# A hybrid decoder block: FOX heads 0 to 3 as a second Strassen stream, and the column steps of the inversions on GpSimd

## The chip, the cores and the metric

The kernel runs on one core of one Trainium2 chip. The metric is the device time of one execution in microseconds (us). Before the change the median of three runs is 983.41 us (983.08 to 984.17).

## What is computed

One decoder block over 512 tokens of width 1024. Two branches read the same normalised input; each has 8 heads of width 128.

```python
u = rmsnorm(x)
gq, gk, gv, gz, ga, gb, fq, fk, fv, ff, gate_a, gate_b = split(u @ w_in)
o_a = gated_delta_rule_chunked(l2norm(silu(conv(gq))), l2norm(silu(conv(gk))), silu(conv(gv)), g, beta)
y_a = (rmsnorm(o_a) * silu(gz)) @ w_proj_gdn            # GDN branch, a triangular solve in each chunk
y_b = forgetting_attention(rmsnorm(fq), rmsnorm(fk), fv, log_f) @ w_proj_fox      # FOX branch
h   = x + (sigmoid(gate_a) * y_a + sigmoid(gate_b) * y_b) @ w_out
out = h + relu(rmsnorm(h) @ w_up)**2 @ w_down
```

## The kernel before

All products are done in pairs of reduced-precision parts: an operand is split into `hi` (a cast, on ScalarE) and `lo` (the rest, a subtraction on VectorE), and three products hi*hi, lo*hi, hi*lo are summed in PSUM. `unit` (line 260) hands out the weight tiles of 128 x 1024 in the order of the list `seq`; it loads them three units ahead and splits them two units ahead (`LA_RAW`, `LA_SPLIT`). The pool `whl` holds four `hi` and four `lo` tiles, so the split of a unit waits until an earlier unit's products are over.

The program is written as a main sequence on TensorE and a set of generators (`tasks`); `tick` advances each of them by one step. A scheduler then fixes one order for each engine, and on the chip each engine works through its own list in that order.

Main sequence around the change, before: 5 `z` units, the 12 units of GDN heads 0 to 3 (`gdn_group(0)`), then `fox_pair(0)` and `fox_pair(1)` for FOX heads 0 to 3, three more `z` units, `gdn_group(1)` with 12 units, and then `stream`: seven Strassen chunks (three for FOX heads 4 to 7, four for the merge gates). Behind it come the projections and the MLP, which the change does not touch.

`fox_pair` (line 950) multiplies in the plain way: a pair of heads takes 3 panels, a panel 4 token blocks, a block 24 matmuls of 256 columns (lines 961, 962, 964). A Strassen chunk (`stream`, line 981) makes the same amount of output, 512 columns of weights over all tokens, out of 7 products P1 to P7 of 24 matmuls of 256 columns (line 1011), where the plain way takes 8 such products. Its weight factors are sums of blocks: P1, P2 and P3 are loaded, and P5, P6, P4 and P7 are made by a DMA that GpSimd issues and that adds to a tile already loaded (line 219). P5 is added onto P1's tile, P6 onto P5's, P4 onto P6's, and P7 onto P3's. Such a DMA waits until the tile's last form has been split (line 257). The sums of `u` that the products P5, P7, P6 and P3 need are made by `factors_u` (line 426), before the change from the end of `fox_pair(0)` on, on VectorE.

In the GDN branch, `group_chain` waits for the four heads of a group and then runs `invert` (line 659). It transposes the diagonal blocks (`E`, line 669), copies an identity (`X`, line 672) and does 31 column steps, each a product into `tmp` (line 681) and a subtraction from `X` (line 683); each of these 62 instructions needs the result of the one before. `X` is then transposed (`Xd`, line 689), and the first matmuls that use it write `Qp` (line 707). The scan of the group follows. The number `INV_STEP` says after how much of this work `invert` yields to the main sequence. `fox_worker` does the attention of one head: a row maximum and sums on VectorE, a power on GpSimd (`rsq`, line 346) and two products on GpSimd that normalise the page `fqk` (line 889).

Of the kernel before, what the change touches and what calls it, by code (L numbers as in the profile page):

```python
# [39 lines left out]
LA_SPLIT = 2  # L40
INV_STEP = (2500, 900)


def hybrid_block(tc, a, out):
# [155 lines left out]
    def load(n):  # L200
        nme, i = seq[n]
        if nme in FACTOR:
            w, c, s_ = i
            q, old = FACTOR[nme]
            if old is None:
                if w == "w_st":
                    raw = (swp if nme == "P1" else wraw).tile([P, D], F32, tag="raw", name=nm("sraw"))
                else:
                    raw = fresh[2 if nme == "P2" else s_].tile([P, D], F32, tag="raw", name=nm("draw"))
                nc.sync.dma_start(raw, a[w][c, q, s_])  # L210
            elif (nme, i) in LONE:
                if n not in begun:
                    begin(n)
                raw = begun[n]
                nc.gpsimd.dma_start(raw, a[w][c, 2, s_], accum_op=ALU.add)
            else:
                raw = factors[old, i]
                assert seq.index((old, i)) < len(units)
                nc.gpsimd.dma_start(raw, a[w][c, q, s_], accum_op=ALU.add)  # L219
# [15 lines left out]
    def prefetch_new(n):  # L235

        for m in range(pos[0], min(len(seq), n)):
            if fresh and m not in raws and seq[m][0] in FACTOR and FACTOR[seq[m][0]][1] is None and seq[m][1][0] != "w_st":
                load(m)
            if seq[m] in LONE and m not in begun:  # L240
                begin(m)
# [39 lines left out]

    def split(src, scale=None, dst=None):

        hi, lo = dst or (page(F32R, "hi")[:, :], page(F32R, "lo")[:, :])
        if scale is None:
            act.copy(hi, src)
            vec.tensor_tensor(lo, src, hi.bitcast(F32), op=ALU.subtract)
        else:
# [370 lines left out]
    def invert(AT, rest, ahead):  # L659
# [11 lines left out]
        X_ = page(s="X")  # L671
        vec.tensor_copy(X_, x_id)
        yield
# [3 lines left out]
        for j in range(B - 1):  # L677
            r, n = B - 1 - j, j // 2 + 1
            tmp = smp.tile([P, 144], F32, tag="tmp", name=nm("tmp"), bufs=2)
            t3 = tmp[:, 0:r * n].rearrange("p (a b) -> p a b", a=r)  # L680
            vec.tensor_tensor(t3, E3[:, j + 1:, j:j + 1].to_broadcast([P, r, n]),
                              X3[:, j:j + 1, 0:n].to_broadcast([P, r, n]), op=ALU.mult)
            vec.tensor_tensor(X3[:, j + 1:, 0:n], X3[:, j + 1:, 0:n], t3, op=ALU.subtract)
            w += 2 * (130 + r * n)
# [153 lines left out]

    def gdn_group(g, box):
        AT = atp.tile([P, NI, P], F32, tag="AT", name=nm("AT"))  # L840
        hd = drp.tile([5, NCH, P, G, P], F32, tag=f"hd{g}", name=f"hd{g}")
        hts = []
        for i in range(G):
            h = g * G + i
            ys = []
            for j in range(3):
                ys.append(project(h, j))
                tick()
            hts.append(start(head(h, AT, *ys, box, hd)))
        return start(group_chain(g, AT, hd, hts))  # L850


    fq = []
    hold = [False]
    taken = [0]
# [10 lines left out]
    def fox_worker(after=None):  # L866
# [3 lines left out]
        while taken[0] < H:  # L870
            if taken[0] >= len(fq) or hold[0]:
                yield
                continue
# [75 lines left out]

    def fox_pair(hp):  # L950
        vts = ([], [])
        for pn in range(3):
            us = [unit("w_fox"), unit("w_fox")]
            pg2 = [page(s="fqk"), page(s="fqk")]
            for t2 in range(2):
                ps = mmps("fx")
                for tb in (2 * t2, 2 * t2 + 1):
                    o = ps[:, (tb % 2) * 256:(tb % 2 + 1) * 256]
                    for k in range(KT):
                        w = us[k // 4][0][:, (k % 4) * 256:(k % 4 + 1) * 256]  # L960
                        mm(o, uhi[k][:, cs(tb)], w, start=(k == 0), stop=False)  # L961
                        mm(o, ulo[k][:, cs(tb)], w, start=False, stop=False)  # L962
                    for k in range(KT):
                        mm(o, uhi[k][:, cs(tb)], us[k // 4][1][:, (k % 4) * 256:(k % 4 + 1) * 256], start=False,  # L964
                           stop=(k == KT - 1))
                    if tb % 2 == 0:
                        tick()
                if pn < 2:
                    act.copy(pg2[t2], ps)
                else:  # L970
                    for j in range(2):
                        (vec.tensor_copy if j else act.copy)(
                            v3(pg2[j][:, 2 * t2 * P:(2 * t2 + 2) * P], 2), v3(ps[:, :], 2)[:, :, cs(j)])
                tick()
            if pn < 2:
                fq.append((2 * hp + pn, pg2, vts[pn]))
            else:
                for v, x in zip(vts, pg2):
                    v += [x[:, cs(c)] for c in range(NCH)]

    def stream(parts, other):

# [11 lines left out]

        for p, c in STREAM:
            if p is None:
# [16 lines left out]
            done = parts[c][2]  # L1013
            at[0] = c
            if p == "P1":
# [85 lines left out]
    finish(fu)  # L1101
    fws += [start(fox_worker()) for _ in range(1, NFW)]


# [36 lines left out]
    parts += [gate_chunk(i, to) for to in (sga, mg) for i in range(2)]  # L1141
    stream(parts, merge_gdn)

# [296 lines left out]
def _layout(inputs):  # L1440
# [20 lines left out]
    fx = w[:, 4112:7184].reshape(D, 3, H, P)  # L1461
    pan = []
    for hp in range(2):
        for h in (2 * hp, 2 * hp + 1):
            pan.append(np.concatenate([fx[:, 0, h], fx[:, 1, h]], axis=1))
        pan.append(np.concatenate([fx[:, 2, 2 * hp], fx[:, 2, 2 * hp + 1]], axis=1))
    o["w_fox"] = c(np.stack(pan).reshape(6, 2, 4, P, 256).transpose(0, 1, 3, 2, 4).reshape(12, P, D))
    q, k, v = [[fx[:, j, h] for h in range(H)] for j in range(3)]
# [51 lines left out]
```

## Time and profile before

| what | value |
|---|---|
| median of the runs | 983.41 us |
| lowest and highest run | 983.08, 984.17 us |
| span of the profiled execution, first to last instruction | 980.2 us |
| instructions in it | 17198 |
| granted TensorE clock | 1.000 |
| TensorE busy | 970.8 us (99%) |
| VectorE, ScalarE, GpSimd busy | 710.9, 605.0, 240.2 us |

In the rows of the profile PE is TensorE, DVE VectorE, ACT ScalarE, POOL GpSimd and SP the engine that issues most loads. The time of the profiled execution itself, as the runs are timed, is not on the page; its span lies 2.9 to 4.0 us under the runs. The profiler gives a matmul a modelled end, so the rate of matmuls is read from rows with a count, and not from the duration of one.

### The profile page before, as it was taken

How to read it: one execution, taken by the hardware profiler on the slowest of the kernel's cores; microseconds unless marked ns; L12 is line 12 of the kernel's file. 1: busy time of each engine (PE TensorE's matmuls, PEld its weight loads, DVE VectorE, ACT ScalarE, POOL GpSimd, SP SyncE). 2: the span in 40 equal slices, each digit the busy share in tenths (PEclk: the TensorE clock that was granted, in tenths of full speed). 3: DMA queues.
4: the chain of work that ended last, by engine and by line, in shares of the span. 5: the costliest groups of instructions: out<-in, count | busy, mean ns of one | idle time of the engine just before them, and what ended most of it. 6: DMA issues, size and time to landing. Idle time of an engine off the chain costs nothing.

```text
span 980.2 us, 17198 instructions
## 1 busy us (share of the span) xinstructions
PE 970.8 (99%) x6545; PEld 874.8 (89%) x6545; DVE 710.9 (73%) x1204; ACT 605.0 (62%) x1050; POOL 240.2 (25%) x236
## 2 busy tenths in 40 slices
PE   8999999999999999999999999999999999999998
PEld 6788899998888999999999888889989989988986
DVE  6877778566577789855656535889896697698596
ACT  7766444766564787867656422678755765666761
POOL 1544120202533513522320005312121121121110
PEclk9999999999999999999999999999999999999999
DMA  7647662475437885757887735688798888889884
GB/s 266 213 135 223 174 158 90 130 239 181 129 116 228 189 166 141 197 129 166 236 201 215 273 103 171 125 181 173 190 188 196 187 173 206 181 175 202 186 166 119
DMA packets 93442, 174.38 MB, mean 178 GB/s; under 512 B 8016, under 2 KB 49200, under 8 KB 93360
## 3 DMA queue, kind: packets, MB, share of 16 engines
q1 hardware_dynamic: 78928, 120.85, 38.8%
q0 software_dynamic: 14432, 52.44, 30.5%
q8 instruction: 51, 0.84, 0.4%
q14 instruction: 31, 0.25, 0.1%
HBM read 152.25 MB, written 21.02 MB: 177 GB/s over the span
## 4 chain that ended last, share of the span: by engine, by line
PE 92%; DVE 4%; DMA 2%; ACT 1%; issue 1%; SPq 0%; DVEq 0%
PE mlp L1171 36%; PE st L1011 12%; PE mm L279 8%; PE mm L276 8%; PE mm L275 8%; PE fx L964 2%; PE fx L961 2%; PE fx L962 2%; PE fo L944 2%; PE sc L919 1%; PE pT L935 1%; DVE lo L257 1%; PE kk L639 1%; PE kq L647 1%; DMA ux<-ud 1%; PE v L797 1%
## 5 line engine op out<-in xcount | busy, mean ns | idle before, releaser
L1402 ACT CAST hi<-draw 128x1024 fp32r<-128x1024 f32 x124 | 130.0, 1050 | 118.4 <-PE mlp L1171 100.4
L1409 DVE TENSOR_TENSOR lo<-draw,hi 128x1024 fp32r<-128x1024 f32 x124 | 151.3, 1222 | 44.8 <-ACT hi L1402 41.6
L256 ACT CAST hi<-raw 128x1024 fp32r<-128x1024 f32 (+1 forms) x62 | 62.9, 1021 | 82.6 <-PE mm L276 59.5
L1171 PE MATMUL mlp<-hi,shi 128*128 128x512 f32 x280 | 109.5, 391 | 0.1
L1171 PE MATMUL mlp<-hi,slo 128*128 128x512 f32 x280 | 109.1, 390 | 0.0
L1171 PE MATMUL mlp<-lo,shi 128*128 128x512 f32 x280 | 109.0, 389 | 0.0
L257 DVE TENSOR_TENSOR lo<-raw,hi 128x1024 fp32r<-128x1024 f32 (+1 forms) x62 | 73.9, 1197 | 29.1 <-ACT hi L256 13.4
L1171 PE MATMUL mlp<-shi,lo 128*128 128x256 f32 x448 | 90.3, 283 | 0.0
L1171 PE MATMUL mlp<-slo,hi 128*128 128x256 f32 x448 | 90.3, 283 | 0.0
L1171 PE MATMUL mlp<-shi,hi 128*128 128x256 f32 x448 | 90.3, 283 | 0.0
L276 PE MATMUL mm<-ulo,hi 128*128 128x512 f32 x216 | 85.0, 394 | 1.2 <-DVE ulo L290 1.2
L275 PE MATMUL mm<-uhi,hi 128*128 128x512 f32 x216 | 85.0, 395 | 0.0
L257 DVE TENSOR_TENSOR lo<-sraw,hi 128x1024 fp32r<-128x1024 f32 x49 | 60.7, 1240 | 20.9 <-ACT hi L256 20.1
L1171 PEld LDWEIGHTS mlp<-shi,hi 128*128 128x128 f32 x448 | 70.6, 192 | 0.9
L1171 PEld LDWEIGHTS mlp<-shi,lo 128*128 128x128 f32 x448 | 69.9, 192 | 0.0
L1171 PEld LDWEIGHTS mlp<-slo,hi 128*128 128x128 f32 x448 | 69.8, 192 | 0.0
L256 ACT CAST hi<-sraw 128x1024 fp32r<-128x1024 f32 x49 | 51.3, 1047 | 26.6 <-PE st L1011 16.2
L1171 PEld LDWEIGHTS mlp<-hi,shi 128*128 128x128 f32 x280 | 52.6, 188 | 11.1 <-issue 0.7
L1171 PEld LDWEIGHTS mlp<-lo,shi 128*128 128x128 f32 x280 | 52.6, 188 | 11.1
L1171 PEld LDWEIGHTS mlp<-hi,slo 128*128 128x128 f32 x280 | 52.6, 188 | 10.3
L219 POOL DMA_DIRECT2D draw<-w_d x30 | 26.3, 876 | 129.9 <-DVE lo L1409 120.8
L219 POOL DMA_DIRECT2D draw<-w_u x32 | 27.7, 866 | 122.6 <-DVE lo L1409 120.0
(336 smaller groups left out, 2466.6 us busy)
## 6 DMA issues: line engine op xcount, KB each, us to landing
draw<-w_u POOLq DMA_DIRECT2D x32, 512.0 KB, 5.7
draw<-w_d POOLq DMA_DIRECT2D x32, 512.0 KB, 6.5
sraw<-w_st POOLq DMA_DIRECT2D x28, 512.0 KB, 5.9
draw<-w_d SPq DMA_DIRECT2D x26, 512.0 KB, 4.4
raw<-w_gdn SPq DMA_DIRECT2D x24, 512.0 KB, 3.8
draw<-w_u SPq DMA_DIRECT2D x24, 512.0 KB, 4.4
sraw<-w_st SPq DMA_DIRECT2D x21, 512.0 KB, 5.5
hd<-hd SPq DMA_DIRECT2D x34, 256.0 KB, 5.4
```

What stands on the lines that cost most here:

```text
L219: nc.gpsimd.dma_start(raw, a[w][c, q, s_], accum_op=ALU.add)
L256: act.copy(hi[:, c], raw[:, c])
L257: vec.tensor_tensor(lo[:, c], raw[:, c], hi[:, c].bitcast(F32), op=ALU.subtract)
L275: mm(o, w, rhi(k), start=(k == 0), stop=False)
L276: mm(o, w, rlo(k), start=False, stop=False)
L279: mm(o, lo[:, k * cols:(k + 1) * cols], rhi(k), start=False, stop=(k == KT - 1))
L944: mm(po[:, cs(i)], vt[c], st[i][:, cs(c)], start=(c == 0), stop=(c == i))
L961: mm(o, uhi[k][:, cs(tb)], w, start=(k == 0), stop=False)
L1011: mm(o, u, w, start=first and t == 0 and k == 0 and j == 0 and x is hi, stop=x is lo and k == 3, skip_group_check=True)
L1171: return (lambda *args, **kw: tc.keep_in_program_order(f(*args, **kw))) if self.pinned[0] else f
L1402: pact.copy(hi, raws[m][0])
L1409: pvec.tensor_tensor(lo, raws[m][0], hi[:, :].bitcast(F32), op=ALU.subtract)
```

## The change

FOX heads 0 to 3 are computed by three Strassen chunks behind the last `z` units, with the new weight array `w_sf`. `fox_pair` and the flag `hold` are gone, and both attention workers start at the beginning. The order of the products is a table, `EARLY`; its two `None` entries stand for two projections of GDN head 4. `factors_u` starts behind the third GDN head. Its sums stand on VectorE in both programs, and the new argument `lo_by` of `split` is given by nobody. In `invert` the 62 column instructions go to GpSimd, the copy of the identity to ScalarE, and a `yield` is added behind the transposes; `INV_STEP` is the same for both groups.

```diff
-INV_STEP = (2500, 900)
+INV_STEP = (1600, 1600)
...
-    seq += [("w_gdn", i) for i in range(12)] + [("w_fox", i) for i in range(12)]
-    seq += [("w_z", i) for i in range(NZ1, H)] + [("w_gdn", 12 + i) for i in range(12)]
+    seq += [("w_gdn", i) for i in range(12)]
+    EARLY = [("P1", 0), ("P2", 0), ("P5", 0), ("P1", 1), ("P3", 0), ("P6", 0), ("P2", 1), ("P7", 0), ("P5", 1), ("P4", 0),
...
+    seq += [("w_z", i) for i in range(NZ1, H)]
+    seq += [(p, ("w_sf", c, 0)) if p else ("w_gdn", 12 + c) for p, c in EARLY]
+    seq += [("w_gdn", 14 + i) for i in range(10)]
...
         X_ = page(s="X")
-        vec.tensor_copy(X_, x_id)
+        act.copy(X_, x_id)
...
-            vec.tensor_tensor(t3, E3[:, j + 1:, j:j + 1].to_broadcast([P, r, n]),
+            pool.tensor_tensor(t3, E3[:, j + 1:, j:j + 1].to_broadcast([P, r, n]),
                               X3[:, j:j + 1, 0:n].to_broadcast([P, r, n]), op=ALU.mult)
-            vec.tensor_tensor(X3[:, j + 1:, 0:n], X3[:, j + 1:, 0:n], t3, op=ALU.subtract)
+            pool.tensor_tensor(X3[:, j + 1:, 0:n], X3[:, j + 1:, 0:n], t3, op=ALU.subtract)
...
     start(decays(0, box, gt))
-    fws = [start(fox_worker())]
-    ch0 = gdn_group(0, box)
-    fox_pair(0)
-    fu = start(factors_u())
-    fox_pair(1)
-    start(decays(1, box, ch0))
-    hold[0] = True
+    fws = [start(fox_worker()) for _ in range(NFW)]
+    fu = []
+    ch0 = gdn_group(0, box, {2: lambda: fu.append(start(factors_u()))})
     for h in range(NZ1, H):
         zgate(h)
-    ch1 = gdn_group(1, box)
-    hold[0] = False
-    finish(fu)
-    fws += [start(fox_worker()) for _ in range(1, NFW)]
+    finish(*fu)
+    v01, v23 = ([], []), ([], [])
+    ahead = []
+    stream([fox_chunk((None, v01), (0, v01[0])), fox_chunk((2, v23[0]), (1, v01[1])), fox_chunk((3, v23[1]), (None, v23))],
+           EARLY, lambda: ahead.append(project(G, len(ahead))), False)
+    start(decays(1, box, ch0))
+    ch1 = gdn_group(1, box, ahead=ahead)
```

Three places show how this moves instructions. All are in the inversion of the first group. TensorE first, where the inversion's result is used; before, the plain FOX products stood ahead of the first `Qp`:

```order
L962 MATMUL fx_2168<-hi_1833,ulo_194 128x256
L964 MATMUL fx_2168<-lo_1828,uhi_179 128x256
L964 MATMUL fx_2168<-lo_1828,uhi_180 128x256
L964 MATMUL fx_2168<-lo_1828,uhi_181 128x256
L707 MATMUL Qp_1875<-Xd_1819,AT_588 32x32
```

Now the last matmuls of P6 of the second chunk stand there (`hi_1972` and `lo_1973` are its weights):

```order
L988 MATMUL st_1682<-hi_1972,hi_1509 128x256 x2
L988 MATMUL st_1682<-hi_1972,lo_1303 128x256 x2
L988 MATMUL st_1682<-hi_1972,lo_1510 128x256 x2
L988 MATMUL st_1682<-lo_1973,hi_1302 128x256 x2
L988 MATMUL st_1682<-lo_1973,hi_1509 128x256 x2
L714 MATMUL Qp_1932<-Xd_1843,AT_588 32x32
```

From the end of the last GDN head's `kq` to `Qp` there stand 8 matmuls of 512 columns and eleven products of 24 matmuls on TensorE. On VectorE, before, the last column steps, then the transpose:

```order
L681 TENSOR_TENSOR tmp_1787<-E_1537,X_1539 128x30
L683 TENSOR_TENSOR X_1539<-X_1539,tmp_1787 128x2x15
L681 TENSOR_TENSOR tmp_1790<-E_1537,X_1539 128x16
L683 TENSOR_TENSOR X_1539<-X_1539,tmp_1790 128x16
L689 STREAM_TRANSPOSE Xd_1819<-X_1539 128x32x16
```

Now the splits of four weight tiles stand ahead of it (`lo_2196` is P7 of the second chunk); the steps are gone to GpSimd:

```order
L893 TENSOR_SCALAR fss_1884<-fss_1884 128x8
L263 TENSOR_TENSOR lo_2073<-sraw_1976,hi_2072 128x1024
L263 TENSOR_TENSOR lo_2130<-sraw_2076,hi_2129 128x1024
L263 TENSOR_TENSOR lo_2196<-sraw_1851,hi_2195 128x1024
L695 STREAM_TRANSPOSE Xd_1843<-X_1515 128x32x16
```

The split `lo_2196` takes the buffer of the P6 whose matmuls stand just ahead of `Qp`: four tiles (P3, P1, P2 and P7, the last of them this one) wait for TensorE behind `Qp`, and the pool has four. On GpSimd, before, no step stands between the products of the attention and the clearing of `X`:

```order
L878 AFFINE_SELECT nd_1481<-row_1479 128x512
L346 TENSOR_TENSOR fss_1485<-fss_1485,expo 128x8
L652 TENSOR_TENSOR conv_1150<-conv_1150,row_1438 128x512
L889 TENSOR_TENSOR fqk_1286<-fqk_1286,fss_1485 128x512
L889 TENSOR_TENSOR fqk_1287<-fqk_1287,fss_1485 128x512
L697 MEMSET X_295_1823 32x16x32
```

Now the steps share the list with the weight DMAs and the attention; the DMA onto `sraw_1542` waits for `lo_1973`, and behind the last row here 19 more steps follow:

```order
L689 TENSOR_TENSOR X_1515<-X_1515,tmp_1715 128x12x10
L225 DMA sraw_1542<-w_sf 128x1024
L687 TENSOR_TENSOR tmp_1718<-E_1513,X_1515 128x121
L352 TENSOR_TENSOR fss_1884<-fss_1884,expo 128x8
L689 TENSOR_TENSOR X_1515<-X_1515,tmp_1718 128x11x11
L225 DMA sraw_1976<-w_sf 128x1024
L897 TENSOR_TENSOR fqk_1750<-fqk_1750,fss_1884 128x512
L897 TENSOR_TENSOR fqk_1662<-fqk_1662,fss_1884 128x512
L687 TENSOR_TENSOR tmp_1752<-E_1513,X_1515 128x110
```

The power `fss_1884` waits for a sum on VectorE that stands there behind `lo_1973`. The second inversion, in the main stream, has the same form: its last 14 steps stand behind two such products and behind a DMA that waits for the split of P1 of the fourth chunk, and the transpose behind the split of P7 of the third chunk, which takes the buffer of the last product ahead of `Qp`.

More of the change, by code (lines that the diff above doesn't have):

```diff
@@ L205, in load @@
             if old is None:
-                if w == "w_st":
+                if w in ("w_st", "w_sf"):
                     raw = (swp if nme == "P1" else wraw).tile([P, D], F32, tag="raw", name=nm("sraw"))
@@ L237, in prefetch_new @@
         for m in range(pos[0], min(len(seq), n)):
-            if fresh and m not in raws and seq[m][0] in FACTOR and FACTOR[seq[m][0]][1] is None and seq[m][1][0] != "w_st":
+            if fresh and m not in raws and seq[m][0] in FACTOR and FACTOR[seq[m][0]][1] is None and seq[m][1][0] not in ("w_st", "w_sf"):
                 load(m)
@@ L280, in dense, with split @@
         return ps
-    def split(src, scale=None, dst=None):
+    def split(src, scale=None, dst=None, lo_by=None):
         hi, lo = dst or (page(F32R, "hi")[:, :], page(F32R, "lo")[:, :])
@@ L286, in split @@
             act.copy(hi, src)
[L287 removed]
+            (lo_by or vec).tensor_tensor(lo, src, hi.bitcast(F32), op=ALU.subtract)
         else:
@@ L694, in invert @@
         XT3 = v3(XT[:, :], NI)
+        yield
         X2 = sbp.tile([P, NI, 64], F32, tag="sub", name=nm("X2"))
@@ L837, in group_chain, with gdn_group @@
         yield from scan(g, AT, hd, got)
-    def gdn_group(g, box):
+    def gdn_group(g, box, between=None, ahead=()):
         AT = atp.tile([P, NI, P], F32, tag="AT", name=nm("AT"))
@@ L846, in gdn_group @@
             for j in range(3):
-                ys.append(project(h, j))
+                ys.append(ahead.pop(0) if ahead else project(h, j))
                 tick()
             hts.append(start(head(h, AT, *ys, box, hd)))
+            if between and i in between:
+                between[i]()
         return start(group_chain(g, AT, hd, hts))
     fq = []
-    hold = [False]
     taken = [0]
@@ L870, in fox_worker @@
         while taken[0] < H:
-            if taken[0] >= len(fq) or hold[0]:
+            if taken[0] >= len(fq):
                 yield
@@ L948, in fox_worker, with stream @@
             stores.append(start(store_late(obd[h], o)))
[L950 to L981, printed above, removed]
+    def stream(parts, order, other, main):
         bank = {}
@@ L993, in to @@
                     vec.tensor_tensor(x, x, ps, op=op)
-        for p, c in STREAM:
+        for p, c in order:
             if p is None:
@@ L1013, in stream @@
             done = parts[c][2]
-            at[0] = c
+            if main:
+                at[0] = c
             if p == "P1":
@@ L1141, in hybrid_block @@
     parts += [gate_chunk(i, to) for to in (sga, mg) for i in range(2)]
-    stream(parts, merge_gdn)
+    stream(parts, STREAM, merge_gdn, True)
     ot2 = start(outputs_in2())
@@ L1461, in _layout @@
     fx = w[:, 4112:7184].reshape(D, 3, H, P)
[L1462 to L1467, printed above, removed]
     q, k, v = [[fx[:, j, h] for h in range(H)] for j in range(3)]
@@ L1471, in _layout @@
     st += [w[:, n + T * i:n + T * i + T] for n in (7192, 8216) for i in range(2)]
-    st = np.stack(st).reshape(7, 2, 4, P, 2, 256)
-    o["w_st"] = c(np.stack([st[:, j, :, :, l] for j, l in ((0, 0), (0, 1), (1, 1), (1, 0))], 1)
-                  .transpose(0, 1, 3, 2, 4).reshape(7, 4, 1, P, D))
+    sf = [np.concatenate(b, axis=1) for b in
+          ((v[0], v[1], q[0], k[0]), (q[2], k[2], q[1], k[1]), (q[3], k[3], v[2], v[3]))]
+    for name, m in (("w_sf", sf), ("w_st", st)):
+        m = np.stack(m).reshape(len(m), 2, 4, P, 2, 256)
+        o[name] = c(np.stack([m[:, j, :, :, l] for j, l in ((0, 0), (0, 1), (1, 1), (1, 0))], 1)
+                    .transpose(0, 1, 3, 2, 4).reshape(len(m), 4, 1, P, D))
     o["w_z"] = units(w[:, 3072:4096])
```

2 lines of the change are left out of this document (added).

## Prediction

> **What bounds the kernel now.** I read the page first, then TensorE's waits, then the stages, then the chain. From the page:
>
> ```profile
> span 980.2 us, 17198 instructions
> PE 970.8 (99%) x6545; PEld 874.8 (89%) x6545; DVE 710.9 (73%) x1204; ACT 605.0 (62%) x1050; POOL 240.2 (25%) x236
> PE 92%; DVE 4%; DMA 2%; ACT 1%; issue 1%; SPq 0%; DVEq 0%
> ```
>
> TensorE is busy for 99% of the span, and 92% of the chain that ended last runs over it. What it waits for (engine, line, releaser: us in total, times, longest):
>
> ```profile
> PE mm L276 <- DVE ulo L290: 1.2, 2, 0.7
> ...
> PE pT L935 <- ACT pTs L937: 0.2, 1, 0.2
> ```
>
> The longest named wait sums to 1.2 us. The stages that the change touches, the plain FOX products and the first three Strassen chunks (window; its length; busy us of PE, PEld, DVE, ACT, POOL; clock):
>
> ```profile
> 123.00:216.00 93.00, 92.52 (x936) 90.26 (x935) 61.85 (x151) 53.99 (x109) 14.26 (x13) 1.00 0.50 147
> 325.00:401.00 76.00, 75.83 (x615) 73.15 (x614) 67.02 (x169) 58.74 (x128) 28.73 (x28) 1.00 0.78 176
> ```
>
> In both, TensorE has no time to give away. VectorE is full in the second one, 67.0 of 76 us, and TensorE still waits for nothing there. So fewer matmuls shorten the kernel one for one, a lighter VectorE brings about nothing, and each new wait of TensorE lengthens the kernel one for one. The span is 980.2 us and the median run 983.41; I carry the 3.2 us around the span over unchanged. Less than 0.2%, 2.0 us, a measurement of this kernel can't tell from no change.
>
> **Part 1, the matmuls.** Rows of the chain (start, us, engine, tile and line, count) and one group:
>
> ```profile
> 124.44 0.96 PE fx L964 x8
> 324.90 2.87 PE st L1011 x24
> L961 PE MATMUL fx<-hi,uhi 128*128 128x256 f32 x192 | 48.5, 288 | 0.0
> ```
>
> Both kinds take 0.12 us per matmul of 256 columns (0.96/8, 2.87/24). There are three lines of 192, 576 in all; 21 products of 24 are 504. The gain is 72 x 0.12 = 8.6 us. All of it is on the path, since TensorE is the bound in that stage.
>
> **Part 2, what feeds them.** 21 weight tiles are split where 12 were, and 12 of them come by DMAs that GpSimd issues.
>
> ```profile
> L256 ACT CAST hi<-sraw 128x1024 fp32r<-128x1024 f32 x49 | 51.3, 1047 | 26.6 <-PE st L1011 16.2 <-DMA sraw<-w_st 8.3 <-PE mm L276 1.4
> L257 DVE TENSOR_TENSOR lo<-sraw,hi 128x1024 fp32r<-128x1024 f32 x49 | 60.7, 1240 | 20.9 <-ACT hi L256 20.1 <-DMA hd<-conv 0.7
> sraw<-w_st POOLq DMA_DIRECT2D x28, 512.0 KB, 5.9
> ```
>
> A link of the factor chain (DMA 5.9, cast 1.05, split 1.24) is 8.2 us, or 2.9 products of 2.87 us. In the order written P5 to P6 is three products, so it just fits, if GpSimd issues at once. The 9 more casts and splits (9.4 us of ScalarE, 11.2 us of VectorE) lie beside TensorE's 60 us of products. Nine loads on SP's queue replace twelve, which costs nothing.
>
> **Part 3, the column steps.** The 62 steps of an inversion are a serial chain. On VectorE (count, duration min/median/max in ns, first and last start):
>
> ```profile
> L681 DVE TENSOR_TENSOR tmp<-E,X x62: 174/262/1020, 143.5 to 399.7; 128x126 f32<-128x126 f32 x6, 128x30 f32<-128x30 f32 x4, 128x56 f32<-128x56 f32 x4, 128x78 f32<-128x78 f32 x4
> ```
>
> No GpSimd row has their shape. The nearest are products of two full tiles of 256 and of 512 columns, and a pair in which the second needs the first:
>
> ```profile
> L1229 POOL TENSOR_TENSOR m<-gate,gate x16: 723/1407/1647, 582.7 to 622.4; 128x256 f32<-128x256 f32 x16
> L652 POOL TENSOR_TENSOR conv<-conv,row x8: 1280/1298/1376, 83.4 to 347.8; 128x512 f32<-128x512 f32 x8
> ...
> 190.59 1.87 POOL L346 TENSOR_TENSOR fss<-fss,expo 128x8 f32<-128x8 f32 x1 [19.78 <-DVE fss L885]
> 192.54 2.04 POOL L889 TENSOR_TENSOR fqk<-fqk,fss 128x512 f32<-128x512 f32 x2
> ```
>
> From the two minima: (1280 - 723)/256 = 2.18 ns a column and 166 ns fixed; the dependent one starts 0.08 us after the end of the other. A step of n columns is then 0.25 us + 2.18 ns x n. By the loop's sizes 62 steps hold 5712 columns: 15.3 + 12.4 = 27.7 us. I bound a step from below by VectorE's median, 0.26 us, and take the line through the two rows, which are GpSimd's own. [...]
>
> The moved steps decide when `Xd` is ready, and TensorE's `Qp` stands in a fixed place. Rows for what lies between:
>
> ```profile
> L346 POOL TENSOR_TENSOR fss<-fss,expo x8: 1637/1932/2714, 139.2 to 437.9; 128x8 f32<-128x8 f32 x8
> L889 POOL TENSOR_TENSOR fqk<-fqk,fss x16: 1032/1057/1346, 142.1 to 442.0; 128x512 f32<-128x512 f32 x16
> 330.64 0.88 POOL L219 DMA_DIRECT2D sraw<-w_st  x1 [1.82 <-DVE ssk L617]
> 331.24 1.33 POOL L346 TENSOR_TENSOR ssk<-ssk,expo 128x4 f32<-128x4 f32 x1
> L689 DVE STREAM_TRANSPOSE Xd<-X 128x512 f32<-128x512 f32 x2 | 2.4, 1182 | 0.0
> 139.10 0.89 PE kq L647 x8
> 106.58 1.81 PE mm L279 x8
> ...
> L448 DVE TENSOR_TENSOR ux<-ux,ux 128x256 f32<-128x256 f32 x12 | 5.3, 481 | 0.1
> ```
>
> A DMA issue takes 0.6 us of GpSimd's time. *First inversion.* GpSimd's list ties its last part to the split of P6 of the second chunk, `lo_1973`: a DMA waits for it, and the power `fss` for a sum queued behind it. From the end of that split: DMA 0.6, step 0.5, power 1.64, step 0.5, DMA 0.6, two products 2.1, the last 20 steps (1400 columns) 4.9 + 3.1 = 8.0, `Xd` 1.2; together 15.1 us. TensorE then has only P4 of the first chunk and 21 matmuls of P6, 45 x 0.12 = 5.4 us, 1.2 of which may already have run under the split. It waits 9.7 to 10.9 us; I take 10. With steps at 0.26 us the chain is 12.0 us and the wait about 6. It can't fall below 3.0: the split ahead of `Xd` needs the buffer of the very last product, so cast (0.5 us of it after the end), split 1.24 and `Xd` 1.18 run with TensorE idle. Does P6 itself come in time? Before, the first step (143.5) came 3.5 us after `kq`'s end (139.99); now a split (1.24) and two sums of `u` (0.48 each) stand ahead, so about 5.7 us. Then 29 steps (2656 columns) 12.9, two DMAs 1.2, landing 5.9, cast 1.05: 26.8 us, and TensorE needs it after 8 matmuls of 512 columns (1.81) and 214 of 256 (214 x 0.12 = 25.7), 27.5 us of work. On time, with 0.7 us of slack. Queued behind the waiting `Qp` on TensorE is everything, and behind the transposes on VectorE the splits.
>
> *Second inversion.* The split of P1 of the fourth chunk waits for P5 of the third: cast and split 2.3, DMA 0.6, two products 2.1, step 0.5, the last 14 steps (772 columns) 5.1, `Xd` 1.2; 11.8 us. TensorE meanwhile has two products, 5.7 us, and 9 `fo` and 7 transposes of the attention.
>
> ```profile
> 196.25 0.89 PE fo L944 x8
> ```
>
> An `fo` is two records of 0.11 us, a transpose one: 2.8 us, 8.5 with the products. It waits 3.3 us, at least the same 3.0, and up to 14 if GpSimd is late by the 10 us of the second rival.
>
> **Part 4, the sums of `u`.** They start earlier, and the products that need them stand close behind. Of the chain before:
>
> ```profile
> 177.15 7.02 DMA ux<-ud
> 184.19 0.72 ACT ux L436
> ```
>
> Loads 7.0 us, four scalings 2.9, then sums and splits, with the second half's loads queued on SP behind a weight load that waits for a split. Before, the products that need them began at 324.90, nearly 150 us behind these loads; now the last `z` units and two or three products lie between. The cost is 0 to 6 us; I take 2, since the needs come spread over four products. The scan of the first group and the decays of the second also start later, but ten more GDN units of 24 matmuls follow (3 x 1.81 = 5.4 us each); I cost them at nothing, and if that cover fails the heads of the second group wait.
>
> **The sum.** 983.4 - 8.6 + 10 + 3.3 + 2 = 990.1, so 990 us, 0.7% slower. Its own range, from the ends above (6 to 11, 3 to 5, 0 to 6): 984 to 997.
>
> **Rivals.** *The waits shrink (faster).* If a step costs less than VectorE's and the work between is early, both waits fall to their floor of 3.0 us and the third to nothing: 983.4 - 8.6 + 6.0 = 980.8; with the buffers freed sooner than I read it, 975. For it: the 25% load of GpSimd over the kernel. Against it: the serial list above. It decides below about 6.6 us of new waits in all. Centre 979. *About equal:* floors and 2 to 3 us for the sums, 983. *The shared port (slower still).* A GpSimd product that starts just after a split on VectorE takes 0.92 us more than the next one, which has none beside it:
>
> ```profile
> 582.58 1.22 DVE L257 TENSOR_TENSOR lo<-raw,hi 128x1024 fp32r<-128x1024 f32 x1
> 582.75 1.64 POOL L1229 TENSOR_TENSOR m<-gate,gate 128x256 f32<-128x256 f32 x1 [64.06 <-DVE gate L1227]
> 584.36 0.72 POOL L1229 TENSOR_TENSOR m<-gate,gate 128x256 f32<-128x256 f32 x1
> ```
>
> If every split stops the chain of steps like this, the first inversion loses 8 x 0.92 = 7.4 us (five splits ahead of the DMA for P6, three behind), less the 0.7 of slack, and the second 11 x 0.92 = 10 us: 990 + 16.7, about 1006. Against it: the minima of L652 and L889 above lie close to their medians, so most GpSimd products meet no split, and the steps are short. [...] *The change does less than it says:* the sums of `u` are on VectorE before too; nothing follows from their name.
>
> **How the numbers follow.** Forecast 0.42 (990); port 0.20 (1006); equal 0.16 (983); faster 0.22 (979). Slower by over 0.2%: 0.42 + 0.20 = 0.62. The range 976 to 1005 leaves out the upper half of the port's case and the fastest of the faster one.
>
> **What would show it.** Right: the chain through POOL and `Xd` just ahead of `Qp` in both inversions, TensorE idle 8 to 11 us at the first and 3 to 5 at the second; steps of 0.2 to 0.5 us on GpSimd; 504 more `st` matmuls at 0.12 us and no `fx`. Wrong: TensorE idle under 6 us in the whole stretch up to the second `Qp`; steps below 0.25 us; or a wait elsewhere, at weight tiles that land late or in the second group's heads.

## The result, and the profile after

The changed kernel takes 1020.78 us in the median (1017.87 to 1024.64, 4 runs), the kernel before 983.25 us in runs beside it (981.35 to 984.17). The ratio is 1.0382 (95% interval 1.0355 to 1.0408): 37.5 us slower, where 990 us were forecast and 1005 us was the upper end. The head of the page of the changed kernel (engine, busy us, share, instructions; then the chain that ended last, and the granted clock in 40 slices):

```profile
span 1019.1 us, 17128 instructions
PE 971.0 (95%) x6473; PEld 872.8 (86%) x6473; DVE 703.1 (69%) x1092; ACT 613.2 (60%) x1059; POOL 316.6 (31%) x372
PEclk9999999699999999989999999999999999999999
PE 78%; POOL 6%; DVE 4%; issue 4%; DMA 3%; ACT 3%; SPq 0%; POOLq 0%; DVEq 0%; ACTq 0%
```

TensorE has 72 matmuls fewer (6473 for 6545) and still 971.0 us of busy time, as before. GpSimd, off the chain before, now carries 6% of it, and in two stretches the granted clock falls below full speed. What TensorE waits for (engine, line, releaser: us in total, times, longest):

```profile
PE Qp L714 <- DVE Xd L695: 22.5, 2, 12.1
PE st L988 <- ACT hi L262: 8.1, 2, 5.6
PE st L988 <- ACT fqk L968: 4.0, 2, 3.1
PE mm L281 <- ACT gate L968: 1.9, 1, 1.9
PE mm L281 <- DVE conv L605: 1.5, 1, 1.5
```

None of these five stood in the list before, where the longest single wait was 1.1 us. Both inversions' `Qp` wait over 10 us for `Xd`, and two Strassen products wait for the cast of a weight tile. Around the two waits at `Qp` (window; length; busy us of PE, PEld, DVE, ACT, POOL; clock; DMA share; GB/s):

```profile
186.00:199.00 13.00, 1.00 (x9) 0.79 (x7) 3.81 (x3) 1.05 (x1) 11.49 (x25) 0.63 0.63 184
199.00:205.00 6.00, 5.91 (x90) 5.84 (x91) 1.45 (x3) 5.81 (x11) 0.00 (x0) 0.66 0.01 3
423.00:434.00 11.00, 0.56 (x7) 0.38 (x7) 4.94 (x3) 0.39 (x2) 9.90 (x22) 0.75 0.50 105
434.00:440.00 6.00, 6.00 (x89) 5.94 (x90) 1.26 (x2) 5.85 (x12) 0.32 (x1) 0.61 0.01 3
```

In the 13 us up to 199 it is mostly GpSimd that works, 11.5 us: two products of the attention (4.1 us), then the last 20 steps. And the wait costs more than its length: in the 6 us behind each, TensorE runs at 0.66 and 0.61 of full clock. The slow clock is most of why its busy time didn't fall.

A whole account can be made from the starts of the matmuls, which are recorded: for each shape of matmul take the median time from one start to the next in the kernel before; summed over all matmuls this is 958.2 us before and 949.6 after (the 8.6 us of the forecast), and what lies over it is 16.7 us before and 64.0 after. The same reckoning place by place gives, with the slow clock behind each wait: 4.9 us at 151 us (a bank that ScalarE empties late, behind a cast of a sum of `u`), 1.2 at 164, 7.1 at 174 (P6's weights), 13.6 at the first `Qp`, 4.3 at 387 (a weight tile), 12.2 at the second `Qp`, and 4.9 in three waits at 313, 558 and 563 us. The five with a slow clock behind them lose 1.3 to 1.6 us each that way, 7.5 together.

How GpSimd's steps look (start, us, engine, line, operation; in brackets the idle time before, and what ended it), first the start of the first inversion, a stretch with a split beside some steps, and the attention's products in its tail:

```profile
149.40 5.21 POOL L687 TENSOR_TENSOR tmp<-E,X 128x31 f32<-128x31 f32 x1 [1.45 <-DMA zd<-proj]
154.68 0.27 POOL L689 TENSOR_TENSOR X<-X,tmp 128x31 f32<-128x31 f32 x1
...
161.87 0.35 POOL L687 TENSOR_TENSOR tmp<-E,X 128x96 f32<-128x96 f32 x1
162.29 1.44 POOL L689 TENSOR_TENSOR X<-X,tmp 128x96 f32<-128x96 f32 x1
...
186.00 4.08 POOL L897 TENSOR_TENSOR fqk<-fqk,fss 128x512 f32<-128x512 f32 x2
```

and what VectorE did at those places:

```profile
162.26 1.22 DVE L263 TENSOR_TENSOR lo<-sraw,hi 128x1024 fp32r<-128x1024 f32 x1 [7.17 <-ACT hi L262]
...
185.17 2.04 DVE L263 TENSOR_TENSOR lo<-sraw,hi 128x1024 fp32r<-128x1024 f32 x1 [2.05 <-ACT hi L262]
```

A product of 96 columns takes 0.35 us, and the subtraction of 96 columns behind it, beside a split, 1.44; the two products of the attention take 4.08 us instead of 2.1, and the split beside them 2.04 instead of 1.22. Both engines hold each other up. The second inversion has the same, here in two steps of one size:

```profile
410.34 0.43 POOL L687 TENSOR_TENSOR tmp<-E,X 128x126 f32<-128x126 f32 x1
410.85 1.30 POOL L689 TENSOR_TENSOR X<-X,tmp 128x126 f32<-128x126 f32 x1
```

### The profile page after: what moved, and what is told of

Read it like the earlier page. It is cut to its first block, busy times and chain, and to the rows that moved or that the text cites. A ratio compares the mean times of both kernels' runs of the same rounds, so it can differ in the third digit from the quotient of the medians.

```text
span 1019.1 us, 17128 instructions
## 1 busy us (share of the span) xinstructions
PE 971.0 (95%) x6473; PEld 872.8 (86%) x6473; DVE 703.1 (69%) x1092; ACT 613.2 (60%) x1059; POOL 316.6 (31%) x372
## 3 DMA queue, kind: packets, MB, share of 16 engines
q0 software_dynamic: 16160, 58.73, 33.2%
## 4 chain that ended last, share of the span: by engine, by line
PE 78%; POOL 6%; DVE 4%; issue 4%; DMA 3%; ACT 3%; SPq 0%; POOLq 0%; DVEq 0%; ACTq 0%
PE mlp L1148 34%; PE st L988 10%; PE mm L281 8%; PE mm L285 8%; PE mm L282 8%; POOL tmp L687 2%; POOL X L689 2%; PE fo L952 1%; PE sc L927 1%; DMA row<-oad 1%; DVE lo L263 1%; DMA sraw<-w_st 1%; ACT hi L262 1%; POOL sraw L225 1%; POOL fqk L897 1%
## 5 line engine op out<-in xcount | busy, mean ns | idle before, releaser
L263 DVE TENSOR_TENSOR lo<-sraw,hi 128x1024 fp32r<-128x1024 f32 x70 | 90.8, 1298 | 64.4 <-ACT hi L262 58.2
L262 ACT CAST hi<-sraw 128x1024 fp32r<-128x1024 f32 x70 | 73.1, 1046 | 75.9 <-PE st L988 23.8
L262 ACT CAST hi<-raw 128x1024 fp32r<-128x1024 f32 (+1 forms) x50 | 50.5, 1014 | 65.2 <-PE mm L282 54.2
L263 DVE TENSOR_TENSOR lo<-raw,hi 128x1024 fp32r<-128x1024 f32 (+1 forms) x50 | 60.8, 1219 | 15.7 <-ACT hi L262 10.3
L988 PE MATMUL st<-hi,hi 128*128 128x256 f32 x320 | 57.3, 298 | 12.1 <-ACT hi L262 8.1
L1148 PEld LDWEIGHTS mlp<-lo,shi 128*128 128x128 f32 x280 | 52.6, 188 | 11.2
```

Source lines behind the costliest of these rows:

```text
L262: act.copy(hi[:, c], raw[:, c])
L263: vec.tensor_tensor(lo[:, c], raw[:, c], hi[:, c].bitcast(F32), op=ALU.subtract)
L988: mm(o, u, w, start=first and t == 0 and k == 0 and j == 0 and x is hi, stop=x is lo and k == 3, skip_group_check=True)
L1148: return (lambda *args, **kw: tc.keep_in_program_order(f(*args, **kw))) if self.pinned[0] else f
```

## The experiments

All are compared with the kernel before on the same chip, whose median in these runs was 982.0 to 982.7 us. Where a kernel leaves work out, its expectation says so.

| run | median us | ratio to before (95%) |
|---|---|---|
| e1_steps_vec | 1008.07 | 1.0261 (1.0247 to 1.0275) |
| e2_plain_pool | 989.71 | 1.0081 (1.0064 to 1.0098) |
| e3_lo_on_act | 1014.77 | 1.0330 (1.0317 to 1.0344) |
| f1_vec_late | 992.21 | 1.0101 (1.0084 to 1.0118) |
| f2_pool_late | 1003.68 | 1.0216 (1.0195 to 1.0238) |
| f3_vec_late_u1 | 996.82 | 1.0144 (1.0124 to 1.0163) |
| f4_pool_late_u1 | 1006.71 | 1.0254 (1.0235 to 1.0272) |
| g1_q_vec | 995.82 | 1.0137 (1.0118 to 1.0156) |
| g2_ucast_vec | 998.42 | 1.0164 (1.0150 to 1.0179) |
| g12_both | 991.26 | 1.0089 (1.0075 to 1.0103) |
| g3_five_tiles | 999.89 | 1.0184 (1.0167 to 1.0201) |
| h1_no_steps | 985.48 | 1.0030 (1.0020 to 1.0040) |
| h2_no_usums | 1000.84 | 1.0186 (1.0169 to 1.0203) |
| h12_neither | 987.33 | 1.0048 (1.0036 to 1.0060) |
| h4_sp_factors | 991.69 | 1.0092 (1.0079 to 1.0105) |
| k1_evict_vec | 996.35 | 1.0149 (1.0127 to 1.0170) |
| k2_split_one | 991.72 | 1.0094 (1.0079 to 1.0108) |

**Which part of the change costs it: the steps, or the order?** The steps go back to VectorE in the changed kernel:

```diff
-            pool.tensor_tensor(t3, E3[:, j + 1:, j:j + 1].to_broadcast([P, r, n]),
+            vec.tensor_tensor(t3, E3[:, j + 1:, j:j + 1].to_broadcast([P, r, n]),
...
-            pool.tensor_tensor(X3[:, j + 1:, 0:n], X3[:, j + 1:, 0:n], t3, op=ALU.subtract)
+            vec.tensor_tensor(X3[:, j + 1:, 0:n], X3[:, j + 1:, 0:n], t3, op=ALU.subtract)
```

> The changed kernel with the 62 column steps of each inversion back on VectorE; all else as changed. Theory A (the loss comes from the steps on GpSimd, which VectorE's two-input instructions hold up, and from the slow TensorE clock behind each wait): 983.25 - 8.6 for the matmuls + 0 to 4 for the sums of u, 975 to 979 us, and TensorE waits under 1 us at either Qp. Theory B (the loss comes from the Strassen order itself: its weight DMAs, its four split tiles, the earlier sums of u): 1005 us or more, with waits of 3 us and over at both Qp.

1008.07 us: neither 975 nor the old loss. 12.7 us come back, 25 us stay, and TensorE still waits 16.7 us at the two `Qp`:

```profile
PE Qp L714 <- DVE Xd L695: 16.7, 2, 10.9
PE st L988 <- ACT fqk L968: 4.4, 2, 3.4
```

So theory A explains a third of the loss, and theory B the larger part. Why VectorE is late with `Xd` is seen from its own groups between `E` and `Xd` (line, operation, count; busy us, mean ns; idle before), in this kernel and in the kernel before:

```profile
149.50:192.20 42.70, 27.48 (x205) 26.87 (x204) 36.60 (x86) 13.80 (x17) 11.10 (x11) 0.82 0.75 165
...
L263 DVE TENSOR_TENSOR lo<-sraw,hi 128x1024 fp32r<-128x1024 f32 x11 | 15.8, 1436 | 4.1 <-PE st L988 3.3 <-ACT hi L262 0.8
L689 DVE TENSOR_TENSOR X<-X,tmp 128x126 f32<-128x126 f32 (+22 forms) x31 | 7.9, 255 | 0.8
L687 DVE TENSOR_TENSOR tmp<-E,X 128x126 f32<-128x126 f32 (+22 forms) x31 | 7.9, 254 | 0.8
```

```profile
143.40:174.70 31.30, 31.30 (x264) 31.30 (x263) 25.63 (x77) 13.73 (x22) 1.47 (x2) 1.00 0.30 86
...
L257 DVE TENSOR_TENSOR lo<-raw,hi 128x1024 fp32r<-128x1024 f32 x6 | 7.3, 1217 | 2.3 <-PE fx L964 2.3
```

The steps are as short as before. But eleven splits (15.8 us) stand among them where six (7.3 us) stood, since a Strassen product wants a new tile each 2.9 us and a pair of plain tiles lasted 11.5. VectorE has 36.6 us of work between `E` and `Xd` instead of 25.6, and the distance of `Qp` on TensorE didn't grow with it (35 us of its work behind the last `kq` before, 33 here).

**The steps on GpSimd, without Strassen.** The same two lines, the other way, in the kernel before.

> The kernel before with only the 62 column steps of each inversion moved to GpSimd; plain products and all else as before. Theory A: slower, 985 to 1000 us, with waits at Qp of 0 to 5 us in the first inversion and 3 to 12 us in the second, and steps of 1.2 us and more wherever a split runs on VectorE. Theory B: 983 us, within 2 us, since the plain products leave the steps room.

989.71 us, 7.0 us slower than before: theory A's number, but not at the place it named. The first `Xd` came late by 0.5 us only, and the second not at all; the longest wait is for the attention's products, which queue behind the steps on GpSimd:

```profile
PE fqT L898 <- POOL fqk L889: 4.2, 1, 4.2
PE Tp L720 <- ACT Q L710: 2.0, 1, 2.0
...
PE Qp L707 <- DVE Xd L689: 0.5, 1, 0.5
```

**VectorE's part in GpSimd's steps.** In the changed kernel the early chunks' `lo` tiles are written by ScalarE:

```diff
-                vec.tensor_tensor(lo[:, c], raw[:, c], hi[:, c].bitcast(F32), op=ALU.subtract)
+                if seq[len(units)][0] in FACTOR and seq[len(units)][1][0] == "w_sf":
+                    act.copy(lo[:, c], raw[:, c])
+                else:
+                    vec.tensor_tensor(lo[:, c], raw[:, c], hi[:, c].bitcast(F32), op=ALU.subtract)
```

> The changed kernel, with the lo parts of the early chunks' weight tiles written by ScalarE as a plain copy of the weights (the subtraction is left out), so that VectorE runs no split of them beside the steps of the first inversion. Theory A: GpSimd's steps there lose their 8.7 us of extra time ahead of the DMA for P6 and some 3.8 us behind it; TensorE's wait for P6 goes from 5.7 us to under 1 and the one at the first Qp from 12.3 to 8 or 9; 1010 us (1005 to 1014). Theory C (GpSimd's steps are slow by themselves or wait for their own list, VectorE has no part in it): 1018 to 1023 us and steps as long as before.

1014.77 us, 6 us less, half of what was expected. The wait for P6 (7.1 with the slow clock) is gone, and in the first inversion no step takes over 0.75 us, as theory A has it. Its products into `tmp`, in the changed kernel and then here (count, duration min/median/max in ns):

```profile
L687 POOL TENSOR_TENSOR tmp<-E,X x31: 217/383/5209, 149.4 to 197.4; 128x126 f32<-128x126 f32 x3, 128x30 f32<-128x30 f32 x2, 128x56 f32<-128x56 f32 x2, 128x78 f32<-128x78 f32 x2
...
L690 POOL TENSOR_TENSOR tmp<-E,X x31: 215/407/752, 151.6 to 189.8; 128x126 f32<-128x126 f32 x3, 128x30 f32<-128x30 f32 x2, 128x56 f32<-128x56 f32 x2, 128x78 f32<-128x78 f32 x2
```

The wait at the first `Qp` is only 1.5 us shorter, 10.6 us. GpSimd stands still for 3.6 us at a DMA that waits for P6's `lo`, with the power, the two products and 18 steps behind it, and TensorE arrives at `Qp` 6 us earlier.

**The pieces by themselves.**

> No block is computed here, only pieces by themselves: 12 column steps of 126 columns on GpSimd, first alone, then beside VectorE's back-to-back subtractions of two SBUF tiles of 1024 columns, beside its copies of one tile, beside subtractions with one input in PSUM, and beside 32x32 transposes; then seven bursts of 90 matmuls of 256 columns on TensorE with six idle gaps between them, of about 2 to 11 us. [...] Theory C: a step takes the same time, within 0.1 us, in all five.

Steps of 126 columns on GpSimd, alone, beside subtractions of two SBUF tiles (SBUF is the memory that holds the tiles, PSUM the one for TensorE's sums), beside copies of one, beside subtractions with an input in PSUM, and beside transposes, one row of each:

```profile
2.39 0.41 POOL L85 TENSOR_TENSOR tmp<-E,X 128x126 f32<-128x126 f32 x1
...
11.12 1.28 POOL L85 TENSOR_TENSOR tmp<-E,X 128x126 f32<-128x126 f32 x1
...
25.04 0.75 POOL L85 TENSOR_TENSOR tmp<-E,X 128x126 f32<-128x126 f32 x1
...
38.55 0.42 POOL L85 TENSOR_TENSOR tmp<-E,X 128x126 f32<-128x126 f32 x1
...
46.18 0.42 POOL L85 TENSOR_TENSOR tmp<-E,X 128x126 f32<-128x126 f32 x1
```

Apart from the first and the last ones the steps of a stretch agree within 0.05 us. Beside the subtractions a step waits until VectorE's current two-input subtraction is over and then runs between two of them: 0.87 us more. Copies of one tile cost 0.34 more; there too one step goes with each VectorE instruction, but a copy takes 0.85 us (12 in 10.20) and a subtraction beside steps 1.37 (8 in 10.99). PSUM inputs and transposes cost nothing (0.42 us for the same step). Why subtractions and copies hold a step up and these do not, no row here shows. No step here was held for longer than one instruction. The 5.21 us of the first step in the changed kernel were: that step ended 0.1 us after a run of seven splits and sums that VectorE worked through without a gap. The same step took 1.07 us beside such a run in the version with a later `Qp` below. Why it found no place between them was seen in one execution only and stays open.

TensorE's bursts of 90 matmuls of 256 columns (10.8 us at full speed), six of the seven, each with the gap ahead of it in brackets:

```profile
5.27 13.27 PE L96 MATMUL acc<-r,w 128*128 128x256 f32 x90
20.58 12.54 PE L96 MATMUL acc<-r,w 128*128 128x256 f32 x90 [2.04 <-ACT r L100]
36.23 11.06 PE L96 MATMUL acc<-r,w 128*128 128x256 f32 x90 [3.11 <-ACT r L100]
51.47 12.56 PE L96 MATMUL acc<-r,w 128*128 128x256 f32 x90 [4.18 <-ACT r L100]
69.28 13.72 PE L96 MATMUL acc<-r,w 128*128 128x256 f32 x90 [5.26 <-ACT r L100]
...
114.48 13.36 PE L102 MATMUL acc<-r,w 128*128 128x256 f32 x90 [10.64 <-ACT r L100]
```

A gap of 5 us and over costs 2.6 to 2.9 us behind it, and shorter ones 0.3 to 1.8, not in order of their length: the gap of 2.04 us cost 1.7 (granted clock 0.87 from 20.0 to 33.2 us), and the longer one of 3.11 us only 0.3 (1.00 from 36 to 48 us). Each gap was measured once, and why the costs differ was not shown.

**The place of `Qp`.** `INV_STEP` says how much of the inversion is written between two yields, so a smaller number puts `Qp` further back in TensorE's order: from 33 and 43 us of its work behind the last `kq` to 58 and 64 to 69 (counted in the traces over every matmul between, at the median of its shape before; the expectations have a few us less). For the second inversion this only undoes a part of the change. Before, with 900 for that group, its `Qp` stood 69 us behind `kq`, and the 1600 of the change had brought it forward by 26 us.

```diff
-INV_STEP = (1600, 1600)
+INV_STEP = (900, 900)
```

> Column steps on VectorE as in the run before, and INV_STEP (900, 900), so that the inversion yields more often and TensorE's first Qp stands behind 56 and 65 us of its own work after the last kq, where 33 and 41 stood. Theory D (Qp stands too early in TensorE's order for the longer list of VectorE): both waits at Qp go, 13.3 and 8.7 us with the slow clock behind them, and little replaces them: 1008 - 21 = 987 us (983 to 991). Theory E (the Strassen stage can't feed TensorE any faster, and the wait only moves to weight tiles): 1000 us or more.

> The changed kernel, steps on GpSimd, with INV_STEP (900, 900): Qp behind 56 and 61 us of TensorE's work. Theory D: the waits at Qp, 13.5 and 12.2 us with the slow clock, go; those for the sums of u (4.9) and for P6 (7.1 and 4.3) stay: 1020.8 - 25 = 996 us (990 to 1001). Theory E: 1010 us or more.

992.21 us with the steps on VectorE, 15.9 less; 1003.68 with the steps on GpSimd, 17.1 less. Theory D has the direction, and two thirds to three quarters of the size. `Qp` is out of the list of waits in both; in the first:

```profile
PE st L988 <- ACT fqk L968: 8.9, 3, 4.6
PE fo L952 <- ACT pTs L945: 2.2, 3, 1.1
PE fqT L906 <- POOL fqk L897: 1.9, 1, 1.9
```

The difference between the two, 11.5 us, is the price of the steps on GpSimd once more (12.7 with the early `Qp`).

**The sums of `u` one head earlier** (`{1:` in place of `{2:` where `gdn_group(0)` is called).

> As the first of these three, with factors_u started one GDN head earlier (behind the second). Theory D, and the wait of 3.6 us at about 151 us into the kernel (6.1 with the slow clock) being that for the sums of u: 6 us less than the first, 981 us (977 to 985). If that wait is for a weight tile or a bank instead: no change from the first.

> As the second, with factors_u started one GDN head earlier. Theory D: 5 us less than the second for the sums of u, and part of the 7.1 us for P6, since VectorE's sums and splits of u no longer stand beside the first steps: 988 us (983 to 994), 4 to 10 us over the version with the steps on VectorE. If GpSimd's steps do no harm once Qp stands later: the same as that version, within 2 us.

Both missed: 996.82 and 1006.71, 4.6 and 3.0 us more instead of 5 to 6 less. The wait of 3.6 us at 151 is gone from the first, but TensorE now waits 4.2 us for `conv` on VectorE in the GDN projections: the sums only changed whom they delay.

**What keeps the mended version 17 us over 975.** TensorE's longest waits there are for a bank of the Strassen products. At the longest, at 362 us, ScalarE (start, us, line, operation) shows why:

```profile
363.93 1.04 ACT L262 CAST hi<-sraw 128x1024 fp32r<-128x1024 f32 x1 [9.26 <-DMA sraw<-w_st]
364.88 0.58 ACT L968 COPY fqk<-st 128x512 f32<-128x512 f32 x1
```

The copy that frees the bank stands behind a cast that waited 9.26 us for a weight DMA. GpSimd had issued three such DMAs between 351.0 and 353.8 us; from issue to landing they took (first row; the second is this kernel from 346 to 364 us, with the DMA engines' busy share, 1.01, as its last number but one):

```profile
DMA to landing us min/median/max: 10.3/12.3/12.9
...
346.00:364.00 18.00, 16.31 (x136) 15.87 (x134) 9.64 (x14) 5.54 (x22) 9.57 (x8) 1.00 1.01 223
```

The median of all the weight DMAs on this queue in this run is 5.8 us. So the tile was late at this place because its load took twice as long there. Four repairs were tried on it, each as an edit of this version: the last product with the decays (`q` times `er`, which waits for `kq`) on VectorE; the casts of the sums of `u` on VectorE; both; five tiles in `whl`.

```diff
-        pool.tensor_tensor(q, q, er, op=ALU.mult)
+        vec.tensor_tensor(q, q, er, op=ALU.mult)
...
-                xh_, xl_ = split(x)
+                xh_, xl_ = page(F32R, "hi")[:, :], page(F32R, "lo")[:, :]
+                vec.tensor_copy(xh_, x)
+                vec.tensor_tensor(xl_, x, xh_.bitcast(F32), op=ALU.subtract)
...
-NPG = 53
+NPG = 49
...
-    whl = ctx.enter_context(tc.tile_pool(name="whl", bufs=4))
+    whl = ctx.enter_context(tc.tile_pool(name="whl", bufs=5))
```

> Steps on VectorE and INV_STEP (900, 900), and now the product of the last queries with their decay (the line that waits for kq) on VectorE too, so that GpSimd's weight DMAs don't queue behind it. Theory F (a bank's eviction stands in ScalarE's list behind a cast that waits for a late weight DMA, and that DMA in GpSimd's list behind the wait for kq): the wait of 4.7 us at 362 us, 7.5 with what follows it, goes: 992 - 7 = 985 us (983 to 988). Theory G (the DMAs themselves are too slow for one product each 2.9 us): 990 to 994.

> Steps on VectorE and INV_STEP (900, 900), and the hi casts of the sums of u on VectorE instead of ScalarE. Theory F: ScalarE's eviction no longer stands behind a cast that waits for VectorE's sum, and the wait of 3.6 us at 151 us, 5.2 with the slow clock, goes: 992 - 5 = 987 us (985 to 989). If VectorE itself is what is late there: 991 to 996, since it gets some 5 us more work.

> Both of these edits. Theory F: 980 us (977 to 984), at last level with the kernel before or under it. Theory G and a late VectorE: 990 or more.

> Steps on VectorE and INV_STEP (900, 900), with five hi and five lo weight tiles instead of four (and 49 pages instead of 53 to make room). Theory F: within 2 us of 992, since what is late is a DMA or a sum, not a free tile. Theory H (a split waits for TensorE to free a tile, and holds VectorE's list): 984 to 988.

995.82, 998.42, 991.26 and 999.89 us: theory F's numbers were missed by 8 to 11 us each, and five tiles, with four pages fewer, were worse. The first two repairs changed the waits they aimed at (the 4.7 us at 362 became two of 2.1 and 2.6, the 3.6 at 151 one of 1.4) and lengthened others, since the scheduler writes all lists anew for any edit. Five tiles alone cost 7.7 us, and an edit below that takes work away costs 8.6. So a difference of under some 9 us between two such versions can't be laid to the edit alone. (The 7.0 and 6 us of e2_plain_pool and e3_lo_on_act lie under that too; what is said of them above rests on the waits and steps in their traces.)

Then whole loads were taken away. Without the 62 steps (the lines of the first diff deleted), without the sums of `u`, without both, and with P4 to P7 loaded plainly on SP's queue:

> Steps on VectorE, INV_STEP (900, 900), and the 62 column instructions of each inversion left out (X stays the identity; the yields stay, so the order of the rest does). This leaves out work of the block. Theory K (VectorE's crowded list, steps beside twice as many splits, is what keeps the time 17 us over the 975 that the matmuls alone would give): 978 to 983 us. Theory L (the Strassen stage is held by its weight tiles and bank evictions, whoever does the steps): 987 to 993.

> Steps on VectorE, INV_STEP (900, 900), and factors_u without its loads, sums and splits: the products take unsummed blocks of u in their place. This leaves out work of the block. If the early sums of u cost what their wait at 151 us shows: 992 - 5 = 987 us (985 to 989). Theory K in the wide sense (any VectorE work taken away there helps): 983 to 986. If they cost nothing, 991 to 993.

> Both left out. Theory K: 974 to 978 us, about what the 72 matmuls fewer give. Theory L: 983 to 988, with waits for weight tiles and banks left in the stages of the early chunks and of the first chunks of the later stream.

> Steps on VectorE, INV_STEP (900, 900), and the weight factors P4 to P7 of the FOX and gate chunks loaded plainly by SP's queue instead of added by GpSimd's (the weights' sums are left out). Theory L with GpSimd's list as the cause: the waits behind late weight DMAs go, 7.5 us at 362 us and some of the rest: 983 to 986. If the DMAs come late for another reason (the split that frees the tile): 990 to 994.

985.48, 1000.84, 987.33 and 991.69 us. Without any steps the kernel is 6.7 us faster than with them on VectorE, and still 3.0 us slower than the kernel before. Theory L holds for the 11 us or so by which that is still over 974; the 7 us of theory K are no more than what new lists alone can cost, and without the sums of `u` the same edit is worth 13.5 us (1000.84 to 987.33). The sums of `u` show no cost here (less work, more time: the new lists make TensorE wait 9.9 us for `conv` on VectorE). GpSimd's queue isn't what makes the DMAs late: issued on SP's, the three at the same place still took 9.2 to 10.6 us to land. What is left without steps:

```profile
PE st L983 <- ACT fqk L963: 6.6, 3, 3.2
```

The last two moved the copies out of the banks to VectorE, and the casts one unit later (`LA_SPLIT` 1).

> Steps on VectorE, INV_STEP (900, 900), and the plain copies out of the Strassen banks (the first eviction of each page) on VectorE instead of ScalarE, so that no bank waits in ScalarE's list behind a cast whose weight DMA is late. Theory L in the form that the place of the eviction is the cause: the waits of 3.6 us at 151 and 4.7 at 362 us go, 984 to 987 us. If the weight tile itself is late: TensorE waits for the cast or the split instead, 990 to 994; VectorE's longer list could also cost as much as this brings.

> Steps on VectorE, INV_STEP (900, 900), and LA_SPLIT 1 instead of 2, so that a tile is cast and split one unit ahead of its use and the casts stand later in ScalarE's list, behind more evictions. Theory L by the place of the eviction: 985 to 989 us. If the tiles themselves come late, a later split makes it worse: 995 or more, with waits for casts and splits all over the stage.

996.35 and 991.72 us; neither helps. With the copies on VectorE the same wait is there under VectorE's name, and longer:

```profile
PE st L988 <- DVE fqk L968: 10.9, 4, 6.1
```

So in these runs the bank's wait isn't a matter of which engine empties it or where the cast stands; tiles or sums that come late hold whatever stands behind them in a list. For the longest of these waits the trace names the slow loads (10.3 to 12.9 us above; 10.2 us also for the tile at 387 in the changed kernel). What makes them slow no run varied, and why tiles and sums are late elsewhere stays open. No version tried beats the kernel before.

## Why the prediction was wrong, point by point

- **Where the loss would show.** Right: TensorE's work fell by the 8.6 us of part 1, and every new wait lengthened the kernel one for one. 47.3 us of new stalls less 8.6 are 38.7; the spans differ by 38.9.
- **The step that failed: the price of a step, and on it P6 "on time, with 0.7 us of slack" and the 3.3 us at the second `Qp`.** The price, 0.25 us + 2.18 ns a column, was right beside an idle VectorE (0.41 and 0.45 us at 126 columns, without the 0.08 between two; the line has 0.44). It was wrong for that place, beside splits, where em_parts has 1.28. From the first step to the end of P6's cast the forecast had 21.0 us; it took 30.2, of which 5.0 are the first step and 3.7 four steps held by a split. The first step also began 8.8 us behind `kq` and not 5.7. So P6's tile came 5.6 us late, although TensorE itself had lost 6.1 us on the way. In the second inversion ten steps were held, 9.9 us together; GpSimd reached the last 14 late, and the wait was 10.4 us. The forecast had priced that case ("up to 14 if GpSimd is late") and not taken it.
- **The first `Qp`.** Its 10 us came out at 12.1, and this chain was read rightly: the last 20 steps took 7.9 us (8.0 forecast), and most of the rest is the attention's two products beside splits, 4.1 us and not 2.1.
- **The rival that the forecast calls the port.** No run shows a port; what the runs show is that GpSimd's steps and VectorE's splits take turns (1.28 us for a step of 0.41 in em_parts; 1.44 and 1.30 us beside splits in the changed kernel). The price was there, with 0.92 us for a split against 0.87 measured in em_parts, and the rival had a chance of 0.20. Its sums for it came out too: 7.4 us forecast and 7.5 found in the first inversion (3.7 ahead of P6's DMA, 3.8 behind, the first step not counted), 10 and 9.9 in the second. What spoke against it, that most products' minima lie near their medians, says only that few of those products met a split; the third row that the forecast shows, L1229, has a minimum of 0.72 us and a median of 1.41, and it spoke for it. In the changed kernel the splits and the steps are in the same stage by design, and that should have made it the likeliest. Its 1006 us were still short: it had no term for the clock (7.5 us), the first step (5.0) or a late tile (4.3).
- **Missing: the clock.** No term had the slow clock behind a wait. It adds 1.3 to 1.6 us to each of five waits here, 7.5 us, and lies in the runs' mean clock of 0.98.
- **Missing: the order of the list.** The forecast read the wait at `Qp` as GpSimd's. With the steps on VectorE, as short as before, it is 16.7 us at the two `Qp` all the same: in the first inversion eleven splits stand between `E` and `Xd` where six did and `Qp` stayed 33 us behind `kq`, and in the second the change had brought `Qp` forward from 69 us to 43, which no term of the forecast names. Part 2 counted those splits as 11.2 us "beside TensorE's products", but they stand in the list on which `Xd` depends. A later `Qp` gives back 16 to 17 us in both pairs of runs.
- **Part 2, the feed, and part 4, `u`.** "It just fits" didn't: 4.3 us at 387 for a tile. The sums of `u` showed 4.9 us at their first use, in the bounds of 0 to 6 (2 were taken); without them the time didn't fall.

By the runs, from 982.7: 8.6 less for the matmuls, to 974.1, which is worked out and not a run; 18.1 for the new stage even in its mended order, 992.2; 15.9 for the early `Qp`, 1008.1; 12.7 for the steps on GpSimd, 1020.8. The last two are each shown by two pairs of runs (17.1 and 11.5 in the other pair). The 18.1 are what is left over: without any steps 11 of them stay, in waits for banks and the slow clock behind them, and how the rest divides is not settled.

## What to carry to other kernels

Where one engine is full, a saving on it is worth its time only if what feeds it gets room as well: a product that needs a new tile each 2.9 us instead of 5.8 puts twice the splits into the lists on which later waits depend, so the place of those waits has to move too. Before work goes to GpSimd, look for what VectorE runs in the same stretch, and price each instruction beside it, not alone (a step of 0.41 us took 1.28 beside subtractions in em_parts). Price a wait of TensorE with the slow clock behind it (1.3 to 1.6 us more at five waits of the changed kernel), and test a repair by what the whole time does, since a wait that is removed from one list often comes back in another.

## What the runs showed of the hardware that was not expected

- In em_parts GpSimd and VectorE take turns instruction by instruction when VectorE subtracts two SBUF tiles: 1.28 us for a step of 0.41. Beside copies of one float32 tile, which are shorter, a step takes 0.75; PSUM inputs and 32x32 transposes cost nothing (0.42).
- It goes both ways, and not always by one instruction. A split that began 0.2 us ahead of GpSimd's two products of 512 columns took 3.64 us instead of 1.22 in e1_steps_vec and ended 1.1 us after both; another, in the changed kernel at 423.6 us, took 3.69:

```profile
179.62 3.64 DVE L263 TENSOR_TENSOR lo<-sraw,hi 128x1024 fp32r<-128x1024 f32 x1 [0.37 <-ACT hi L262]
```

```profile
176.48 2.76 POOL L352 TENSOR_TENSOR fss<-fss,expo 128x8 f32<-128x8 f32 x1
179.21 0.89 POOL L225 DMA_DIRECT2D sraw<-w_sf  x1
179.84 2.32 POOL L897 TENSOR_TENSOR fqk<-fqk,fss 128x512 f32<-128x512 f32 x2
```

- In em_parts a gap of 2.04 us on TensorE cost 1.7 us of slow clock behind it (0.87 from 20.0 to 33.2 us), and one of 3.11 us only 0.3 (1.00 from 36 to 48 us).
